# Two passes or one for small transposes, paired 64x64 products, a factor moved into u, and products of ones at the start of a hybrid decoder step

## The chip, the cores and the metric

The kernel runs on one core of a Trainium2 chip. The metric is the device time of one execution in microseconds (us), the median of repeated runs. The traces come from the hardware profiler, one execution each.

## The reference, cut to what matters

One layer of a decoder runs over 16 meta tokens and 512 prompt tokens, and over 8 sample sequences of 4 tokens (560 rows in all, width 1024):

```python
h = rms_norm(x, g_mix); proj = h @ w_in          # 1024 -> 8208
# branch A: GLU -> causal depthwise conv (31 taps) -> LayerNorm -> swish -> w_cout
# branch B: conv (4 taps) + SiLU on q, k, v, then for each of 8 heads, in chunks of L tokens:
M = beta[..., :, None] * einsum('id,jd->ij', k, k) * decay
A = tril(M, -1) + eye(L)
sol = triangular_solve(A, concat([v * beta, k * (beta * exp(G))]))   # value, kcum
attn = einsum('id,jd->ij', q, k) * decay
u = value - kcum @ S                              # S: state, key x value, 128 x 128
o = q_dec @ S + attn @ u
S = S * last + k_dec.T @ u
# o -> per-head RMSNorm * SiLU(z) -> w_dout
mix = sigmoid(gate_c) * conv_out + sigmoid(gate_d) * dn_out
x = x + mix @ w_o;  x = x + square(relu(rms_norm(x, g_mlp) @ w_up)) @ w_down;  y = rms_norm(x, g_final)
```

## The kernel before

**Big products.** Everything is kept transposed, channels on partitions. Each weight tile of 1024x128 is split into a rounded high part `wh` and a rest `wl` (both in fp32r), the activations likewise, and every product of the two is taken as high x high, high x low and low x high. These are the instructions of L613 (88 column tiles in the order of `gemm_order()`: k first, then the GLU pairs, q, v, z, the gates, then `do`, `co`, `wo`), of L2083 (`w_up`) and of L2234 (`w_down`). I call them main products. The weights come by SP's queue into `wraw`; ScalarE rounds them into `wh`. For tiles 12 to 71 ScalarE then writes -wh into `wl` (L579) and a DMA of GpSimd's queue adds the raw weights on top (L581); for the others VectorE subtracts (L585).

**Order.** A planner in the kernel (`Weaver`) writes the order of instructions of every engine when the program is built. The work is written as streams (Python generators) that yield one step at a time with its engine, an estimated cost and what it depends on; the planner always issues the step that could start first by its own clocks, and a priority breaks ties. Each engine then runs its list strictly in order. So a changed cost, dependency or priority moves instructions on all engines. `W.patience` holds back the convolution's VectorE steps (L1217), `tab` names the activation table that a ScalarE step needs.

**Start.** The eight tiles of x (`xs[:, k]`) arrive by DMA. Each is squared (L351 on GpSimd or VectorE, L354 on ScalarE), and TensorE sums the squares over partitions with a column of ones (`column_sums`, L877). Beside that, each tile is split into high and low (L401, L403), and the first four column tiles of the big product run on the split x before the norm is known. `warm` (L300) gives 20 products of ones at the very start and 12 at the end.

**Delta rule.** Gram products of k (L978) fill `KT`; VectorE inverts the 32x32 blocks (`solve`); `doubling` joins blocks to 64 and then to 128 with small products. Its last step has 32 products on rows 0 to 63 of the array (L1108), their move to SBUF, 32 products on rows 64 to 127 (L1119), and their move. For each head, `head_prep` brings v and k of the sample (`v4`, `k4`: L1411, L1413) and of the prompt (L1452, L1461) into token order, and `chain` goes through four chunks of 128 tokens: key and query times S (L1503, L1505), R on VectorE (L1509), T times R (L1518), eviction to `u` on ScalarE (L1520), `kd` times u and `at` times u (L1522, L1525), the new S on VectorE (L1529). A product in `head_post` (L1669) turns the sample's output back. `st["s"]` holds beta over the squared norm of k; `at` is attn times s (L1473, four instructions a head) and `kd` carries `st["sk"]` = s times the decay. `decode_state` updates the sample's states and loads the next by DMA (L1599).

Small products take plain fp32 operands. One such product is one row in the program's order and two rows (two passes) in the trace; the instruction `nc.tensor.transpose` is one row in both.

Of the kernel before, what the change touches and what calls it, by code (L numbers as in the profile page):

```python
# [22 lines left out]
NPH = NPOST // 2  # L23
# [84 lines left out]
class Weaver:  # L108
# [8 lines left out]
    def __init__(self):  # L117
        self.clk = {"pe": 0.0, "dve": 0.0, "act": 0.0, "pool": 0.0, "sp": 0.0}
        self.tab = None

        self.patience = 0.0
        self.streams = []
        self.n = 0
# [16 lines left out]
    def run(self):  # L140
        while self.streams:
            best = None
            moved = False
            for s in list(self.streams):
# [26 lines left out]
            if tab is not None:  # L171
# [18 lines left out]
def build(tc, i, o):  # L190
# [15 lines left out]
    with ExitStack() as ctx:  # L206
# [73 lines left out]
        A0, A1 = 12, 72  # L280
        SQ = "pdapadpd"
        NWARM, NTAIL = 20, 12
# [12 lines left out]
        def warm(n):  # L295

            b, kb, tb = yield from get_bank()
            w = ones[:].bitcast(mybir.dt.bfloat16)
            for _ in range(n):
                nc.tensor.matmul(b[:, 0:256], w[:, 0:128], w, start=True, stop=True)  # L300
            put_bank(kb, tb)

        def start():
# [39 lines left out]
            b, kb, tb = yield from get_bank()  # L343
            ta = [0.0] * 8
            for k in range(8):
# [9 lines left out]
                ta[k] = yield from column_sums(b, sq, ones[:, 0:32], t, tb, start=k == 0, stop=k == 7)  # L355
            b2, kb2, t = yield from sums_to_tokens(b, kb, M0[:, 6984:7112], M0[:, 7112:7160], ta[7],
# [235 lines left out]
        def gemm():  # L592
            src_of = {"do": "o", "co": "c", "wo": "m"}
            for idx, (kind, c) in enumerate(seq):
# [7 lines left out]
                for part in (0, 1):  # L602
                    for k in range(8):
# [6 lines left out]
                        for w, x in ((wls, hi),) if part else ((whs, hi), (whs, lo)):  # L610
                            t = yield op("pe", 2 * N * 0.4605e-3, tp, tk, tf)
# [377 lines left out]
        def kfin(t):  # L989
# [3 lines left out]
            t = yield op("dve", 0.2, t)  # L993
            nc.vector.tensor_tensor(st["sk"][:], st["s"][:], st["ed"][:], op=ALU.mult)
# [54 lines left out]
        def doubling(t0):  # L1049
# [56 lines left out]
            for m in range(32):  # L1106
                t = yield op("pe", 0.058, tn[m // 16], tb)
                nc.tensor.matmul(B[m // 8][64:128, m % 8, :], KT[0:64, m, 64:128], Tn[0:64, m, :], start=True, stop=True)  # L1108
                if m % 8 == 7:
                    tb_.append(t)  # L1110
            t1 = []
            for q in range(4):
                t1.append((yield from move(("act", "dve")[q % 2], 512, tb_[q], P2[q // 2][64:128, 8 * (q % 2):8 * (q % 2) + 8, :],
                                           B[q][64:128])))
            tb_ = []
            for m in range(32):
                h2 = m // 16
                t = yield op("pe", 0.058, *t1[2 * h2:2 * h2 + 2], *tc_[2 * h2:2 * h2 + 2])
                nc.tensor.matmul(B[m // 8][0:64, m % 8, :], P2[m // 16][64:128, m % 16, :], CTT[64:128, m, 64:128],  # L1119
                                 start=True, stop=True)  # L1120
                if m % 8 == 7:
                    tb_.append(t)
            for q in range(4):
# [264 lines left out]
        def head_prep(hh):  # L1388
# [21 lines left out]
            yield op("pe", 0.22, tv, tb4)  # L1410
            nc.tensor.matmul(b4[:96, 0:128], M2["v4"], ident, start=True, stop=True)  # L1411
            yield op("pe", 0.22, tv, tb4)
            nc.tensor.matmul(b4[:wk, 128:256], k4, ident, start=True, stop=True)  # L1413
# [14 lines left out]
            if hh == 5:  # L1428
                W.patience = 0.45
            t = yield op("dve", 0.15, t4)  # L1430
            nc.vector.scalar_tensor_tensor(at4[:48, 0:48], b4[:48, 384:432], st["s"][:48, hh, 4:5], D4[:, hh, :],
                                           op0=ALU.mult, op1=ALU.mult)
# [4 lines left out]
            nc.scalar.activation(kd[32:48, 4, :], b4[32:48, 128:256], AF.Copy, scale=st["sk"][32:48, hh, 4:5])  # L1437
# [3 lines left out]
            for r in (0, 32):  # L1441
                tx = yield op("act", 0.25, t4)
                nc.scalar.activation(kx[r:r + 32], b4[:32, 128:256], AF.Copy, scale=st["sk"][:32, hh, 4:5])
            t = yield op("dve", 0.2, tx)
            nc.vector.scalar_tensor_tensor(kx[64:96], b4[:32, 128:256], st["sk"][:32, hh, 4:5], kx[0:32].bitcast(F32),
# [1036 lines left out]
```

## Time and profile before

| | |
|---|---|
| median of 3 runs | 1069.06 us (1068.16 to 1070.02) |
| the profiled execution | 1068.65 us |
| its span, first to last instruction | 1066.9 us |
| TensorE busy | 1048.2 us (98% of the span) |
| VectorE busy | 769.4 us (72%) |
| ScalarE busy | 622.9 us (58%) |
| GpSimd busy | 148.1 us (14%) |

The span leaves out 1.75 us of the profiled execution. Matmuls are pipelined: a row's duration reaches from its start to the end of its last result, and neighbours overlap, so the cost of a product is read from the distance of the starts and not from its duration.

### The profile page before, as it was taken

To read this page: it belongs to the slowest core of one execution; us is meant where nothing else is said; L and a number is where in the kernel's file an instruction comes from. 1 tells how busy PE (TensorE), PEld (TensorE's weight loads), DVE (VectorE), ACT (ScalarE), POOL (GpSimd) and SP (SyncE) were. 2 spreads that over 40 slices of the span, in tenths; PEclk is the share of its full clock that TensorE was granted. 3 is DMA by queue.
4 is the path that set the end of the run, shared out by engine and by line. 5 is a ranking of instruction groups with operands and counts; after the bars stand their busy time and mean duration, and the time that the engine had idled before them with its cause. 6 is when DMAs were issued, how large, how long until landed. Compare 5 with 4: busy or idle time off the path is not lost.

```text
span 1066.9 us, 21819 instructions
## 1 busy us (share of the span) xinstructions
PE 1048.2 (98%) x8835; PEld 1026.1 (96%) x8835; DVE 769.4 (72%) x1360; ACT 622.9 (58%) x1285; POOL 148.1 (14%) x173
## 2 busy tenths in 40 slices
PE   8999999999999999999999999999999999999997
PEld 6988999999999999899999999999999999999996
DVE  5888879788889887788953355778657547746754
ACT  5677334668787878776358424578327426723741
POOL 2067311102211221122111000000000000000000
PEclk9999999999999999999999999999999999999998
DMA  6232687467576566667877522654365365346222
GB/s 213 82 89 70 124 178 164 87 148 161 139 172 164 143 137 156 164 166 182 187 163 158 179 84 91 163 153 117 109 177 129 100 153 149 94 124 164 80 61 84
DMA packets 57872, 145.55 MB, mean 136 GB/s; under 512 B 14612, under 2 KB 20140, under 8 KB 57772
## 3 DMA queue, kind: packets, MB, share of 16 engines
q1 hardware_dynamic: 46828, 104.32, 30.4%
q0 software_dynamic: 10944, 39.85, 23.2%
q8 instruction: 69, 1.13, 0.4%
q14 instruction: 31, 0.25, 0.1%
HBM read 135.14 MB, written 9.01 MB: 135 GB/s over the span
## 4 chain that ended last, share of the span: by engine, by line
PE 87%; DVE 5%; ACT 3%; DMA 3%; issue 2%; SPq 0%; POOL 0%; POOLq 0%; DVEq 0%; ACTq 0%
PE pg L613 42%; PE pg L2234 17%; PE bk L2083 15%; DVE acc L815 1%; DMA pre<-in_sq_dram 1%; DVE V L1217 1%; PE pg L2083 1%; PE bk L1419 1%; PE bk L1518 1%; PE bk L978 1%; DVE of L815 1%; PE bk L1522 1%; PE bk L1503 1%; DMA M<-in_xT_dram 1%; PE bk L1525 1%
## 5 line engine op out<-in xcount | busy, mean ns | idle before, releaser
L613 PE MATMUL pg<-R,wh 128*128 128x280 f32 (+2 forms) x1920 | 279.3, 295 | 1.0 <-ACT pre L803 1.0
L613 PEld LDWEIGHTS pg<-R,wh 128*128 128x128 f32 x1920 | 253.7, 189 | 3.9 <-issue 1.5
L1217 DVE SCALAR_TENSOR_TENSOR V<-V,vec,V 128x512 f32<-128x512 f32 x240 | 180.5, 781 | 2.2
L568 ACT ACTIVATE wh<-wraw 128x1024 fp32r<-128x1024 f32 (+1 forms) x89 | 93.4, 1049 | 94.3 <-PE pg L613 79.3
L613 PE MATMUL pg<-R,wl 128*128 128x280 f32 (+2 forms) x960 | 144.0, 294 | 0.3 <-issue 0.3
L613 PEld LDWEIGHTS pg<-R,wl 128*128 128x128 f32 x960 | 128.5, 189 | 1.8 <-issue 1.4
L581 POOL DMA_DIRECT2D wl<-in_w_dram x60 | 52.6, 876 | 343.8 <-ACT wl L579 252.5
L2014 ACT ACTIVATE whm<-RT 128x512 fp32r<-128x512 f32 x73 | 45.2, 625 | 53.0 <-PE pg L2234 34.8
L579 ACT ACTIVATE wl<-wh 128x1024 fp32r<-128x1024 f32 x60 | 63.5, 1058 | 14.8 <-PE pg L613 12.9
L1969 POOL DMA_DIRECT2D RT<-in_wu_dram x16 | 13.8, 865 | 381.6 <-DMA RT<-in_wu_dram 185.6
L2017 DVE TENSOR_TENSOR wlm<-RT,whm 128x512 fp32r<-128x512 f32 x73 | 49.8, 687 | 16.9 <-issue 8.4
L2234 PE MATMUL pg<-RD,whm 128*128 128x272 f32 (+2 forms) x272 | 57.7, 288 | 0.0
L2234 PE MATMUL pg<-K,whm 128*128 128x272 f32 (+2 forms) x272 | 57.6, 288 | 0.0
L2083 PE MATMUL bk<-R,whm 128*128 128x272 f32 x318 | 54.5, 288 | 0.0
L613 PE MATMUL pg<-K,wh 128*128 128x272 f32 x256 | 53.0, 289 | 0.2 <-DVE K L1766 0.2
L613 PE MATMUL pg<-RD,wh 128*128 128x272 f32 x256 | 53.2, 289 | 0.0
L2234 PE MATMUL pg<-RD,M 128*128 128x272 f32 x264 | 46.2, 288 | 0.0
L2014 ACT ACTIVATE whm<-wrawm 128x512 fp32r<-128x512 f32 x43 | 26.7, 623 | 32.6 <-PE pg L2234 29.7
L2083 PEld LDWEIGHTS bk<-R,whm 128*128 128x128 f32 x318 | 45.6, 189 | 0.0
L585 DVE TENSOR_TENSOR wl<-wraw,wh 128x1024 fp32r<-128x1024 f32 x28 | 35.1, 1253 | 13.5 <-ACT wh L568 9.5
L2234 PE MATMUL pg<-RD,wlm 128*128 128x272 f32 (+2 forms) x272 | 43.5, 289 | 0.0
L2234 PEld LDWEIGHTS pg<-K,whm 128*128 128x128 f32 x272 | 43.5, 188 | 0.0
(524 smaller groups left out, 2442.5 us busy)
## 6 DMA issues: line engine op xcount, KB each, us to landing
wraw<-in_w_dram SPq DMA_DIRECT2D x87, 512.0 KB, 3.8
wl<-in_w_dram POOLq DMA_DIRECT2D x60, 512.0 KB, 5.6
RT<-in_wu_dram SPq DMA_DIRECT2D x24, 512.0 KB, 5.2
RT<-in_wu_dram POOLq DMA_DIRECT2D x16, 512.0 KB, 7.3
wrawm<-in_wn_dram SPq DMA_DIRECT2D x16, 512.0 KB, 3.6
RT<-in_wn_dram SPq DMA_DIRECT2D x16, 512.0 KB, 3.5
M<-in_sd_dram SPq DMA_DIRECT2D x16, 256.0 KB, 3.4
out_osd_dram<-M SPq DMA_DIRECT2D x16, 256.0 KB, 3.8
```

Of the source, the lines that this page charges most:

```text
L568: nc.scalar.activation(wh[:, c[0]:c[1]], w[:, c[0]:c[1]], AF.Copy)
L579: nc.scalar.activation(wl, wh.bitcast(F32), AF.Copy, scale=-1.0)
L581: nc.gpsimd.dma_start(wl, i["w"][n].bitcast(F32R), accum_op=ALU.add)
L585: nc.vector.tensor_tensor(wl, w, wh.bitcast(F32), op=ALU.subtract)
L613: nc.tensor.matmul(pt[:, hf, 0:N], w[idx][:, k, :], x[:, off + hf * N:off + hf * N + N], start=k == 0 and not part and x is hi, stop=k == ...
L815: nc.vector.scalar_tensor_tensor(acc[:, 0:584], pr[:, q:q + 584], vcol(w + q), acc[:, 0:584], op0=ALU.mult, op1=ALU.add)
L1217: nc.vector.scalar_tensor_tensor(cc[:, 0:512], G[r][:, 16 + q:528 + q], vcol(w + q), cc[:, 0:512], op0=ALU.mult, op1=ALU.add)
L1969: nc.gpsimd.dma_start(rb, i["wu"][g][:, 1024:2048], accum_op=ALU.add)
L2014: nc.scalar.activation(hi, raw, AF.Copy)
L2017: nc.vector.tensor_tensor(lo, raw, hi.bitcast(F32), op=ALU.subtract)
L2083: nc.tensor.matmul(acc[an], w[:, kp, :], x, start=kp == 0 and not part and x is hi and m not in (3, 6, 7), stop=kp == 3 and part == 1, ski ...
L2234: nc.tensor.matmul(out, w[:, k % 4, :], x[:, a], start=n_ == 0 and x is hi, stop=n_ == len(STEPS) - 1)
```

## The change

It has these parts:

- `v4`, `k4` (for seven heads; the eighth has only 48 columns and stays) and the sample's output are turned by `nc.tensor.transpose` and no longer by a product with the identity.
- `doubling`'s last step is written in quarters of 8 products. The second products of quarter 0 alternate with the first products of quarter 2, those of quarter 1 with the first of quarter 3.
- The factor s leaves `at` and `kd` and is put on `u` when it is evicted; `at` becomes one instruction of 512 columns a head, the step that made `sk` goes.
- In `chain` the products with S of an odd chunk use other columns of the bank, so that they no longer wait for the output's eviction.
- `fill` puts four products of ones behind the column sums of each of the first six tiles of x.
- The planner counts 0.09 us more for a main product that follows a small product; `decode_state` gets priority -2 for 1; tiles 64 to 71 have `wl` from VectorE and not from ScalarE and a DMA; the reciprocals of the MLP's norm wait for an earlier product.

```diff
@@ Weaver.run
+                if eng == "pe":
+                    key, switch = (start, s[0], s[1]), False
+                    if best is None or key < best[0]:
+                        best = (key, s, eng, start, cost + (0.09 if self.small and tab == "main" else 0.0), tab)
+                    continue
...
-        A0, A1 = 12, 72
+        A0, A1 = 12, 64
-        NWARM, NTAIL = 20, 12
+        NWARM, NTAIL, NFILL = 20, 12, 6
...
+        def fill(b, n=4):
             w = ones[:].bitcast(mybir.dt.bfloat16)
             for _ in range(n):
                 nc.tensor.matmul(b[:, 0:256], w[:, 0:128], w, start=True, stop=True)
...
                 ta[k] = yield from column_sums(b, sq, ones[:, 0:32], t, tb, start=k == 0, stop=k == 7)
+                if k < NFILL:
+                    t = yield op("pe", 0.43, ta[k], tw_)
+                    fill(bw)
...
-            nc.vector.tensor_tensor(st["sk"][:], st["s"][:], st["ed"][:], op=ALU.mult)
@@ doubling
+            for q in (0, 1):
+                for m in range(8 * q, 8 * q + 8):
+                    yield from first(m, 0.116)
+                yield from keep(q)
+            for q in (2, 3):
+                for m in range(8 * q, 8 * q + 8):
+                    yield from first(m, 0.07)
+                    yield from second(m - 16, 0.07)
+                yield from keep(q)
+                yield from done(q - 2)
+            for q in (2, 3):
+                for m in range(8 * q, 8 * q + 8):
+                    yield from second(m, 0.116)
+                yield from done(q)
@@ head_prep
-            nc.tensor.matmul(b4[:96, 0:128], M2["v4"], ident, start=True, stop=True)
+            nc.tensor.transpose(b4[:96, 0:128], M2["v4"], ident)
-            nc.tensor.matmul(b4[:wk, 128:256], k4, ident, start=True, stop=True)
+            if wk > 64:
+                nc.tensor.transpose(b4[:wk, 128:256], k4, ident)
...
-                nc.scalar.activation(kd[:, j, :], b[:, 128 * j:128 * j + 128], AF.Copy, scale=st["sk"][:, hh, j:j + 1])
+                nc.scalar.activation(kd[:, j, :], b[:, 128 * j:128 * j + 128], AF.Copy, scale=st["ed"][:, hh, j:j + 1])
-            for j in range(4):
-                t1 = yield op("dve", 0.263, t)
-                nc.vector.scalar_tensor_tensor(at[:, j, :], b[:, 128 * j:128 * j + 128], st["s"][:, hh, j:j + 1],
-                                               Ds[hh][:, j, :], op0=ALU.mult, op1=ALU.mult)
+            t1 = yield op("dve", dve_c(512), t)
+            nc.vector.tensor_tensor(at, b.rearrange("p (t c) -> p t c", c=128), Ds[hh], op=ALU.mult)
@@ chain
+                ba, bu = (bx[:, 256:384], bx[:, 0:128]) if j % 2 else (bx[:, 0:128], bx[:, 256:384])
-                nc.scalar.activation(u, bx[:, 256:384], AF.Copy)
+                nc.scalar.activation(u, bu, AF.Copy, scale=st["s"][:, hh, j:j + 1])
...
-            W.spawn(decode_state(hh, tu), 1)
+            W.spawn(decode_state(hh, tu), -2)
@@ head_post
-            nc.tensor.matmul(b4[:, 0:48], ob[:, 4, :], ident[:, 0:48], start=True, stop=True)
+            nc.tensor.transpose(b4[:, 0:128], ob[:, 4, :], ident)
```

What the planner makes of it on TensorE's list at three places. First the start, where `bk` is the bank of the column sums and `pg` the first big product (`V` high, `RT` low part of x). Before:

```order
L877 MATMUL bk_38_149<-M_98,ones_71 32x128 x3
L877 MATMUL bk_38_149<-M_98,ones_71 32x176
L613 MATMUL pg_102<-V_37_148,wh_101 128x280 x2
L613 MATMUL pg_102<-RT_147,wh_101 128x280 x2
L877 MATMUL bk_38_149<-M_98,ones_71 32x128 x3
L877 MATMUL bk_38_149<-M_98,ones_71 32x176
```

And of the change (L895 is the former L877, L631 the former L613, L313 the products of ones):

```order
L895 MATMUL bk_38_149<-M_98,ones_71 32x128 x3
L895 MATMUL bk_38_149<-M_98,ones_71 32x176
L313 LDWEIGHTS ones_71
L313 MATMUL bk_39_150<-ones_71 128x256
L313 LDWEIGHTS ones_71
L313 MATMUL bk_39_150<-ones_71 128x256
L313 LDWEIGHTS ones_71
L313 MATMUL bk_39_150<-ones_71 128x256
L313 LDWEIGHTS ones_71
L313 MATMUL bk_39_150<-ones_71 128x256
L631 MATMUL pg_102<-V_37_148,wh_101 128x280 x2
L631 MATMUL pg_102<-RT_147,wh_101 128x280 x2
```

Four products of ones now stand between the sums of a tile and what follows. Second, the last step of `doubling` (`KT` and `P2` lie in `M`, the inverse in `RT`, each `bk` is a quarter). Before:

```order
L613 MATMUL pg_2349<-R_29_97,wh_2082 128x280 x4
L1108 MATMUL bk_155_2339<-M_751 64x64 x8
L1108 MATMUL bk_156_2340<-M_751 64x64 x8
L1108 MATMUL bk_157_2341<-M_751 64x64 x8
L1108 MATMUL bk_158_2342<-M_751 64x64 x8
L613 MATMUL pg_2349<-R_29_97,wh_2082 128x280 x12
L1119 MATMUL bk_155_2339<-RT_750,M_751 64x64 x8
L1119 MATMUL bk_156_2340<-RT_750,M_751 64x64 x8
```

And of the change (L1128 is the former L1108, L1133 the former L1119):

```order
L631 MATMUL pg_2261<-R_29_97,wh_2102 128x280 x18
L1128 MATMUL bk_158_2392<-M_815 64x64 x8
L631 MATMUL pg_2261<-R_29_97,wh_2102 128x280 x2
L1128 MATMUL bk_159_2393<-M_815 64x64 x8
L631 MATMUL pg_2261<-R_29_97,wh_2102 128x280 x2
L1128 MATMUL bk_160_2394<-M_815 64x64
L1133 MATMUL bk_158_2392<-RT_814,M_815 64x64
L1128 MATMUL bk_160_2394<-M_815 64x64
L1133 MATMUL bk_158_2392<-RT_814,M_815 64x64
```

Two blocks of 32 products have become six blocks: two of 8, two of 8 pairs, two of 8, with main products between them. Third, the first steps of a head's preparation and a post step, where the change issues as many rows as before but other instructions. Of the change:

```order
L1443 MATMUL bk_168_2600<-cst_68,M_2542 96x128
L1446 MATMUL bk_168_2600<-cst_68,kq_26_93 96x128
L1450 MATMUL bk_168_2600<-kq_26_93 96x48
L631 MATMUL pg_2493<-R_29_97,wl_2260 128x274 x2
L1454 MATMUL bk_168_2600<-ones_71,M_2542 128x1 x4
L1454 MATMUL bk_168_2600<-ones_71,M_2542 96x1
...
L631 MATMUL pg_3182<-R_29_97,wl_3065 128x280 x6
L1702 MATMUL bk_198_3285<-cst_68,M_2542 128x128
L631 MATMUL pg_3182<-R_29_97,wl_3065 128x280 x6
```

Here L1443 and L1446 stand for the former L1411 and L1413, and L1702 for L1669, whose moving operand had 48 columns. In all of TensorE's list a main product follows a small one 183 times before and 186 times in the change.

## Rows read from the trace of the kernel before

**Rows 1.** The page: busy time of TensorE, and its busy tenths over 40 slices.

```profile
PE 1048.2 (98%) x8835; PEld 1026.1 (96%) x8835; DVE 769.4 (72%) x1360; ACT 622.9 (58%) x1285; POOL 148.1 (14%) x173
...
PE   8999999999999999999999999999999999999997
```

**Rows 2.** Waits of TensorE: engine, line, waited for: us in total, times, longest.

```profile
PE bk L1503 <- ACT M L1537: 2.1, 2, 1.5
PE bk L1546 <- DMA M<-in_sd_dram: 1.1, 1, 1.1
PE pg L613 <- ACT pre L803: 1.0, 1, 1.0
PE bk L755 <- ACT D L715: 0.8, 1, 0.8
PE bk L755 <- ACT RD L764: 0.6, 1, 0.6
```

**Rows 3.** A window: stretch, length, busy PE, PEld, DVE, ACT, POOL, clock, DMA.

```profile
360.00:400.00 40.00, 39.99 (x341) 38.72 (x340) 33.98 (x74) 33.18 (x102) 10.36 (x9) 1.00 0.65 148
```

**Rows 4.** Timeline of TensorE in head 0's preparation: start, duration, instruction, count.

```profile
206.00 0.38 PE L1411 MATMUL bk<-cst,M 128*96 128x128 f32 x2
206.22 0.38 PE L1413 MATMUL bk<-cst,kq 128*96 128x128 f32 x2
...
209.48 0.60 PE L1452 MATMUL bk<-cst,M 128*128 128x128 f32 x4
209.84 0.37 PE L613 MATMUL pg<-R,wh 128*128 128x274 f32 x1
```

**Rows 5.** Timeline of TensorE at a product of `head_post`.

```profile
289.92 0.32 PE L1669 MATMUL bk<-cst,M 128*128 128x48 f32 x2
290.05 2.05 PE L613 MATMUL pg<-R,wh 128*128 128x280 f32 x14
```

**Rows 6.** Timeline of TensorE around the first products of the last doubling step.

```profile
190.01 0.29 PE L613 MATMUL pg<-R,wh 128*128 128x280 f32 x1
190.23 3.94 PE L1108 MATMUL bk<-M 64*64 64x64 f32 x64
194.10 1.82 PE L613 MATMUL pg<-R,wh 128*128 128x280 f32 x12
```

**Rows 7.** Timeline of TensorE in an earlier doubling step, two quadrants in turn.

```profile
178.83 0.19 PE L1077 MATMUL bk<-M 32*32 32x32 f32 x1
178.83 0.19 PE L1075 MATMUL bk<-M 32*32 32x32 f32 x1
178.86 0.19 PE L1077 MATMUL bk<-M 32*32 32x32 f32 x1
```

**Rows 8.** Windows of the start, columns as in rows 3.

```profile
11.60:14.90 3.30, 3.30 (x20) 2.49 (x18) 3.30 (x4) 3.25 (x6) 1.35 (x1) 0.50 1.02 396
15.00:25.30 10.30, 10.30 (x114) 8.21 (x112) 4.70 (x8) 4.10 (x13) 1.23 (x2) 1.00 0.23 68
```

**Rows 9.** Timeline of TensorE: products of ones at the end of the program.

```profile
1055.89 1.47 PE L300 MATMUL bk<-ones 128*128 128x256 bf16 x12 [0.42 <-DVE V L2301]
```

**Rows 10.** Timelines of TensorE and ScalarE: one chunk's way from T times R to `kd` times u.

```profile
355.91 0.39 PE L1518 MATMUL bk<-M,RT 128*128 128x128 f32 x2
...
357.11 0.39 PE L1522 MATMUL bk<-M 128*128 128x128 f32 x2
...
356.34 0.28 ACT L1520 ACTIVATE M<-bk 128x128 f32<-128x128 f32 x1 [0.37 <-PE bk L1518]
```

**Rows 11.** Groups by line in the heads' stage (200 to 480 us), ScalarE and VectorE.

```profile
L1512 ACT ACTIVATE M<-bk,st_eG 128x128 f32<-128x128 f32 x24 | 8.8, 365 | 9.4 <-DVE M L1509 9.4
L1520 ACT ACTIVATE M<-bk 128x128 f32<-128x128 f32 x32 | 8.7, 271 | 4.8 <-PE bk L1518 4.6
...
L1629 DVE TENSOR_TENSOR M<-bk,M 128x512 f32<-128x512 f32 x14 | 9.6, 684 | 2.4 <-ACT M L1626 2.4
L1473 DVE SCALAR_TENSOR_TENSOR M<-bk,st_s,RD 128x128 f32<-128x128 f32 x32 | 9.5, 344 | 2.0 <-PE bk L1469 2.0
```

More of the change, by code (lines that the diff above doesn't have):

```diff
@@ L119, in __init__ @@
         self.tab = None
+        self.small = False
         self.patience = 0.0
@@ L170, in run @@
             _, s, eng, start, cost, tab = best
-            if tab is not None:
+            if eng == "pe":
+                self.small = tab != "main"
+            elif tab is not None:
                 self.tab = tab
@@ L343, in start @@
             b, kb, tb = yield from get_bank()
+            bw, kw, tw_ = yield from get_bank()
             ta = [0.0] * 8
@@ L610, in gemm @@
                         for w, x in ((wls, hi),) if part else ((whs, hi), (whs, lo)):
-                            t = yield op("pe", 2 * N * 0.4605e-3, tp, tk, tf)
+                            t = yield op("pe", 2 * N * 0.4605e-3, tp, tk, tf, tab="main")
                             for hf in range(2):
@@ L1105, in doubling, with first, second, keep @@
             tb = max(x[2] for x in bks)
-            for m in range(32):
-                t = yield op("pe", 0.058, tn[m // 16], tb)
+            t1, tb_ = [None] * 4, [None] * 4
+            def first(m, cost):
+                tb_[m // 8] = yield op("pe", cost, tn[m // 16], tb)
                 nc.tensor.matmul(B[m // 8][64:128, m % 8, :], KT[0:64, m, 64:128], Tn[0:64, m, :], start=True, stop=True)
[L1109 to L1119, printed above, removed]
+            def second(m, cost):
+                q = m // 8
+                tb_[q] = yield op("pe", cost, t1[q], *tc_[2 * (m // 16):2 * (m // 16) + 2])
+                nc.tensor.matmul(B[q][0:64, m % 8, :], P2[m // 16][64:128, m % 16, :], CTT[64:128, m, 64:128],
                                  start=True, stop=True)
-                if m % 8 == 7:
-                    tb_.append(t)
-            for q in range(4):
+            def keep(q):
+                t1[q] = yield from move(("act", "dve")[q % 2], 512, tb_[q], P2[q // 2][64:128, 8 * (q % 2):8 * (q % 2) + 8, :],
+                                        B[q][64:128])
+            def done(q):
                 t = yield from move(("act", "dve")[q % 2], 512, tb_[q], CTT[0:64, 8 * q:8 * q + 8, 64:128], B[q][0:64], -1.0)
@@ L1531, in chain @@
                     to = yield op("dve", 0.2, to)
-                    nc.vector.tensor_tensor(ob[:, j, :], bx[:, 0:128], tm, op=ALU.add)
+                    nc.vector.tensor_tensor(ob[:, j, :], ba, tm, op=ALU.add)
                 else:
@@ L1536, in chain @@
                     to = yield op("act", 0.17, to)
[L1537 removed]
+                    nc.scalar.activation(ob[:, j, :], ba, AF.Copy)
                 S = Sn
@@ L1885, in mlp_norm @@
             evac_done(n, t)
-            yield wait(("upm", 4, 4))
+            yield wait(("upm", 3, 2))
             for q in range(4):
@@ L2231, in dn_product @@
                 for w, x in ((wl, hi),) if part else ((wh, hi), (wh, lo)):
-                    t = yield op("pe", sum(a.stop - a.start for _, a in parts) * 0.4605e-3, tp, tk, tf)
+                    t = yield op("pe", sum(a.stop - a.start for _, a in parts) * 0.4605e-3, tp, tk, tf, tab="main")
                     for out, a in parts:
```

50 lines of the change are left out of this document (25 added, 25 removed).

## The prediction, written before the changed kernel ran

> **What bounds the kernel now.** I read the page first, for the shares: TensorE is busy for 1048.2 of 1066.9 us, and in 38 of 40 slices its tenths stand at 9 [rows 1]. VectorE and ScalarE stay under three quarters. So the time is TensorE's list plus its gaps, and an edit counts only if it takes something off that list, shortens a wait of TensorE or makes one. Next come TensorE's waits. Above half a microsecond there are few, and those inside the program that I use later come to 5.6 us: 2.1 for the products with S (L1503), 1.1 for a sample's state from DMA (L1546), 1.0 for a big product behind ScalarE (L613), 0.8 and 0.6 for the decay products (L755) [rows 2]. Third, a window of the heads' stage, where the change makes most of its edits: VectorE 34 and ScalarE 33 of 40 us, TensorE all 40 [rows 3]. These engines have some 6 us of slack in 40, so the sources of small products are ready just in time there. Last, timelines at each place touched. In them the reader is to look at the first column, since distances of starts are what a product costs.
>
> **Transposes.** A product with the identity takes two passes: L1411 starts at 206.00 and L1413 at 206.22. A transpose takes one: the four of L1452 reach from 209.48 to 209.84, 0.09 us each. The rows of the instructions say so too, with x2 for one product and x4 for four transposes [rows 4]. The change turns 8 `v4` and 7 `k4` products into transposes, 15 × 0.11 = 1.65 us. The eight of L1669 stand alone between main products, and there the row is cheaper: from its start to the next main product 0.13 us, for both passes of 48 columns [rows 5]. It becomes one pass of 128 columns. Its gain is at most 0.13 and at least nothing, if a lone pass costs as much; I take 0.10, since the way in and out seems to be overlapped already, times 8 = 0.8. Sum **-2.45 us** (bounds -1.65 to -2.7).
>
> **Doubling.** The first block of 32 products reaches from 190.23 to 194.10, where the next main product starts. 64 passes lie in it: 3.94 less some 0.22 for the last pass's own duration (it is 0.19 for a 32x32 one [rows 7]), over 63 distances, is 0.059 us a pass [rows 6]. All 64 products are 128 passes. No row of before has 64x64 products of two quadrants in turn. The nearest is an earlier doubling step with 32x32 quadrants in turn: both rows of a pair start at 178.83, the next pair at 178.86 [rows 7]. There a partner costs nothing. In the change 16 pairs hide 16 products, or 32 passes, 32 × 0.059 = -1.89 us. Against that, there are six blocks where there were two. The edge of a block into main products reads 0.22 us on the way in, 190.01 to 190.23 [rows 6], which is 0.09 above the 0.13 that a main product costs from start to start (2.05 us for 14 [rows 5], less the 0.29 of a single one [rows 6], over 13 distances). On the way out, the last of the 64 passes is done with its distance at 190.23 + 64 × 0.059 = 194.01, and the main product starts at 194.10: 0.09 as well. Four more blocks at 0.18 cost 0.72. Net **-1.2 us**; bounds are -1.9 (edges free) and +0.7 (no overlap of the pairs).
>
> A rule speaks against this part. The Trainium skill, page "TensorEngine Tiling (Array Packing)", section "Key Properties", says that a change of the tiling mode, not just of the tile, drains TensorE; six blocks mean twelve changes for four. The trace agrees that an edge costs something, with the 0.09 read above, and no run yet shows whether a full drain can be longer.
>
> **Products of ones.** At the program's end twelve of them last 1.47 us; less 0.27 for the last one's lag that is 0.109 each [rows 9]. The change adds 24, or 2.6 us. Before, TensorE's clock in 11.6 to 14.9 stood at 0.50, the lower of its two levels (1.2 GHz), after stretches in which it waited for squares and copies, while VectorE and ScalarE were busy for 3.30 and 3.25 of 3.30 us; from 15.0 on it is 1.00 [rows 8]. So until 14.9 TensorE follows the split of x, and fills there fall mostly into its idle time. If the fills raise the clock earlier, a few of the 20 products in that stretch come sooner; but what follows needs the norm, which comes from VectorE and ScalarE. Bounds: -0.8 (a quarter of the slow stretch) and +0.9 (the eight fills of the fifth and sixth tile, 8 × 0.109, are all on the path). I take **0**.
>
> **s in u.** On ScalarE the eviction to `u` gets a factor per row. The row of such an eviction is L1512, 365 ns against the 271 ns of L1520 [rows 11], +0.094 us for 32 chunks and 8 samples, 3.8 us of ScalarE. On VectorE four instructions of 344 ns become one of 512 columns, as L1629 has at 684 ns: 8 × (4 × 0.344 - 0.684) = 5.5 us less [rows 11]. Is the eviction on the path? T times R starts at 355.91, ScalarE evicts from 356.34 to 356.62, and `kd` times u starts at 357.11, with main products between [rows 10]. That leaves some 0.49 us of cover, and +0.094 fits in it. The one `at` instruction comes once a head, before the chain starts, so the chain's first product with `at` waits for 0.684 us of VectorE and no longer for 0.344; it stands several products into the chain. **0 us**; without the cover it would be up to 3.8 us.
>
> **The rest.** For tiles 64 to 71 ScalarE loses eight instructions and GpSimd's queue eight transfers, VectorE gets eight subtractions; main products are waited for by nobody there who is late. The bank's halves swapped in odd chunks take away a wait that the waits don't show. The state's step at -2, the reciprocals one product earlier, the dropped `sk`: each moves work that main products hide now. **0 us** together. The planner's 0.09 moves small products into longer bundles or out of them; TensorE's list has 183 returns from small to main before and 186 in the change, so it saves no edges. 0 too, but see the rivals.
>
> **Sum.** -2.45 - 1.2 = -3.65 us. The profiled execution had 1068.65, of which the span is 1066.9; 1068.65 - 3.65 = 1065.0. That execution lay 0.41 below the median of 1069.06, so the median is forecast at **1065.4 us**. What a measurement of this kernel can tell from no change is about 0.2%, or 2.1 us.
>
> **Rivals.** *Faster, waits go too.* The waits for the decay products (0.8 + 0.6), for ScalarE ahead of L613 (1.0) and for the sample's state (1.1) add to 3.5 us [rows 2]. The earlier priority of the state's step, which issues the next state's load, speaks to the last one, and a less loaded VectorE to the others. If all go, 1065.4 - 3.5 = 1061.9. Against it: other waits take their place easily when the order of everything changes.
>
> *No gain.* TensorE is shortened by 3.65 us, but the engines behind it are not, and those 6 us of slack in 40 [rows 3] are a mean; saved passes turn into waits for VectorE, ScalarE or weights. Waits of 5.6 us [rows 2] would need to grow by two thirds. It gives some 1069.
>
> *Slower, the chain loses its cover.* The planner now believes that each return from small to main costs 0.09 us, on some 140 of the 186 returns (those in the heads' stage), and plans the other engines' steps by a TensorE list 140 × 0.09 = 12.6 us longer than before. The real return, as L1669 shows with 0.13 us for two passes and the way back [rows 5], need not cost that much. Then TensorE arrives earlier than planned at products whose source is not ready. With `u` 0.094 later on top, a hop from T times R to `kd` times u is short by 0.19 us at worst, over 40 hops 7.6 us: 1065.4 + 7.6 = 1073.0. It comes out slower than before by more than a measurement's 2.1 us once the 40 hops wait for 0.14 us each (5.7 us). The 0.49 us of cover speaks against it; the full VectorE and ScalarE of that stage speak for it.
>
> **Chances.** The forecast 0.50, with a range of its own of 1063.7 to 1068.1 (1069.06 with the best bounds, -2.7 - 1.9 - 0.8, and with the worst of transposes and doubling, -1.65 + 0.7); the faster rival 0.20; no gain 0.18; the slower rival 0.12. The forecast and the faster rival end below 1066.9, that is 0.2% under the median, but for 0.05 of the former; the no-gain case ends within 0.2% but for 0.01, and 0.01 of the slower rival does too: faster 0.65, same 0.23, slower 0.12. The range reaches from 1061.0, a little below the faster rival, to 1070.0, above the no-gain case, and leaves out most of the slower rival and a tail of the faster one, together under 0.2.
>
> **What would show it.** Each step has its place in the profile after. The rows of L1443, L1446 and L1702 should have one pass each and 0.09 to 0.12 us to the next start. L1128 and L1133 should start in pairs, 0.12 us from pair to pair of two passes each, in six blocks with edges near 0.09 us. The clock in 11.6 to 14.9 tells what the fills do, and the start of the first product behind the norm tells whether that counts. `u` should last some 365 ns with no wait of TensorE for it above half a microsecond in total, and `at` be one instruction of 684 ns. I am wrong on the forecast if TensorE's waits for the evictions to `u`, for R or for the state's update grow to some 3 us or more, if pairs start 0.06 us apart from partner to partner, or if the edges cost several tenths.

## The result and the profile after

The changed kernel takes 1077.36 us in the median of 5 runs (1075.65 to 1081.27), the kernel before 1069.84 on the same chip. The ratio is 1.0079 with a 95% interval of 1.0057 to 1.0101: slower by 8 us, where 1065.4 was forecast. The profiled execution is the slowest of the five (1081.27); a second profile (e1) spans 1078.4 us. I therefore call structural only what both show.

The busy times on the page of the changed kernel, against [rows 1]:

```profile
PE 1054.0 (98%) x8836; PEld 1029.1 (95%) x8836; DVE 771.8 (71%) x1343; ACT 620.2 (57%) x1278; POOL 140.6 (13%) x165
```

TensorE's five longest waits (engine, line, waited for: us in total, times, longest), against [rows 2]:

```profile
PE bk L1551 <- ACT M L1545: 3.9, 3, 3.5
PE pg L631 <- DVE R L482: 2.7, 3, 1.5
PE bk L1108 <- issue: 2.0, 1, 2.0
PE pg L2267 <- DVE V L2283: 1.7, 1, 1.7
PE pg L2116 <- DVE V L2175: 1.5, 1, 1.5
```

L1551 is T times R in the chain, and its wait is for a ScalarE eviction. The R that L631 waits for is another one: the tiles with the split of the normalized x (L482). L1108 is a 32x32 product of `doubling`. Of these five, before has only the first, with 0.3 us. They add to 11.8 us; the waits of before for the products with S and for in_sd, 3.2 us [rows 2], are gone or small (0.4). They cost more than their length, because the clock falls behind some of them. Windows (columns as in [rows 3]) just behind the waits for R and inside the 32x32 products:

```profile
52.00:56.00 4.00, 3.05 (x12) 2.79 (x13) 4.00 (x5) 1.02 (x2) 2.61 (x2) 0.61 0.23 78
56.00:60.00 4.00, 4.00 (x20) 4.00 (x19) 3.54 (x5) 3.47 (x10) 0.00 (x0) 0.54 0.04 7
196.00:200.00 4.00, 4.00 (x49) 3.96 (x40) 2.98 (x5) 1.18 (x2) 0.00 (x0) 0.57 0.44 88
```

In 56 to 60 TensorE is busy all the time and starts 20 products, where e1 starts 32 and 33 in the two stretches of 4 us from 54 on, with a granted clock of 1.00. Near 0.5 is the lower of the two levels, 1.2 GHz. The fall is not the same in every execution: e1 is the same program with the same waits for R, and there the clock falls behind the stall at L1108 and the wait at L1551 but not behind R. Up to 1040 us the clock's records have the lower level for 13.7 us in the changed kernel, 10.2 in e1, 3.4 before and none in e2. At half the clock half of that is lost, which is an estimate of 5 to 7 us out of the 17 to 18 between e2's profile and these two.

Where the time goes is easiest seen by counting main products, of which all kernels have the same 7104 in nearly the same order. How much later (us) than in the profile of before the n-th starts, counted from the traces' records (an earlier small product in the order also makes the n-th later: ahead of 300, the changed kernel and e5 have 39 small passes more than before and e6 has 15; ahead of 900 it is 24, the products of ones, and none):

| n | 300 | 900 | 1200 | 2700 | 4350 | 7050 |
|---|---|---|---|---|---|---|
| place | R split | before the Gram part | after doubling | after the heads | in the MLP | near the end |
| after | 9.3 | 4.2 | 5.6 | 9.5 | 9.5 | 13.1 |
| after again (e1) | 6.3 | 3.2 | 5.8 | 9.6 | 9.5 | 11.6 |
| e2: neither | -0.8 | -0.8 | -1.6 | -5.9 | -5.9 | -4.7 |
| e5: products, no 0.09 | 6.0 | 2.2 | 8.1 | 3.4 | 3.4 | 5.0 |
| e6: 0.09, no products | 10.3 | 5.3 | 6.6 | 11.3 | 11.3 | 13.7 |
| e7: products, order kept | -0.1 | -0.0 | 2.0 | -3.4 | -3.4 | 1.0 |
| e12: the same, fewer passes | 0.1 | 0.1 | -0.1 | -4.5 | -4.5 | -2.5 |

### The profile page after: what moved, and what is told of

It is laid out like the page before. It is cut to its first block, busy times and chain, and to the rows that moved or that the text cites. A ratio compares the mean times of both kernels' runs of the same rounds, so it can differ in the third digit from the quotient of the medians.

```text
span 1079.5 us, 21784 instructions
## 1 busy us (share of the span) xinstructions
PE 1054.0 (98%) x8836; PEld 1029.1 (95%) x8836; DVE 771.8 (71%) x1343; ACT 620.2 (57%) x1278; POOL 140.6 (13%) x165
## 4 chain that ended last, share of the span: by engine, by line
PE 89%; DVE 3%; ACT 3%; DMA 3%; issue 2%; POOL 1%; SPq 0%; POOLq 0%; DVEq 0%; ACTq 0%
PE pg L631 46%; PE pg L2267 17%; PE bk L2116 14%; DMA RT<-in_wu_dram 1%; PE bk L996 1%; PE bk L1503 1%; PE bk L1555 1%; PE bk L1551 1%; POOL um L1649 1%; DMA M<-in_sd_dram 1%; PE bk L1454 1%; PE bk L1558 1%; DMA M<-in_xT_dram 1%; PE bk L1536 0%; PE pg L2116 0%
## 5 line engine op out<-in xcount | busy, mean ns | idle before, releaser
L631 PE MATMUL pg<-R,wh 128*128 128x280 f32 (+2 forms) x1920 | 282.9, 296 | 2.8 <-DVE R L482 2.7
L631 PEld LDWEIGHTS pg<-R,wh 128*128 128x128 f32 x1920 | 256.7, 191 | 6.8 <-DVE R L482 3.4
L1249 DVE SCALAR_TENSOR_TENSOR V<-V,vec,V 128x512 f32<-128x512 f32 x240 | 173.3, 750 | 3.4 <-ACT V L1240 1.1
L631 PE MATMUL pg<-R,wl 128*128 128x280 f32 (+2 forms) x960 | 144.4, 297 | 0.0
L631 PEld LDWEIGHTS pg<-R,wl 128*128 128x128 f32 x960 | 129.7, 191 | 0.8 <-issue 0.6
L599 POOL DMA_DIRECT2D wl<-in_w_dram x52 | 45.6, 877 | 340.4 <-ACT wl L597 244.4
L603 DVE TENSOR_TENSOR wl<-wraw,wh 128x1024 fp32r<-128x1024 f32 x36 | 45.6, 1266 | 35.6 <-PE pg L631 14.4
L597 ACT ACTIVATE wl<-wh 128x1024 fp32r<-128x1024 f32 x52 | 55.1, 1059 | 12.5 <-PE pg L631 10.2
L2267 PE MATMUL pg<-RD,whm 128*128 128x272 f32 (+2 forms) x272 | 57.7, 288 | 1.7 <-DVE V L2283 1.7
L2267 PE MATMUL pg<-K,whm 128*128 128x272 f32 (+2 forms) x272 | 57.7, 288 | 0.0
L2116 PE MATMUL bk<-R,whm 128*128 128x272 f32 x318 | 54.5, 288 | 0.0
L631 PE MATMUL pg<-K,wh 128*128 128x272 f32 x256 | 53.2, 289 | 0.2 <-DVE K L1799 0.2
L631 PE MATMUL pg<-RD,wh 128*128 128x272 f32 x256 | 53.0, 288 | 0.0
L2267 PE MATMUL pg<-RD,M 128*128 128x272 f32 x264 | 46.2, 288 | 0.0
L2116 PEld LDWEIGHTS bk<-R,whm 128*128 128x128 f32 x318 | 45.5, 188 | 0.0
L2267 PEld LDWEIGHTS pg<-RD,whm 128*128 128x128 f32 x272 | 43.4, 188 | 1.9 <-issue 1.9
L2267 PE MATMUL pg<-RD,wlm 128*128 128x272 f32 (+2 forms) x272 | 43.4, 288 | 0.0
```

What stands on the lines that cost most here:

```text
L597: nc.scalar.activation(wl, wh.bitcast(F32), AF.Copy, scale=-1.0)
L599: nc.gpsimd.dma_start(wl, i["w"][n].bitcast(F32R), accum_op=ALU.add)
L603: nc.vector.tensor_tensor(wl, w, wh.bitcast(F32), op=ALU.subtract)
L631: nc.tensor.matmul(pt[:, hf, 0:N], w[idx][:, k, :], x[:, off + hf * N:off + hf * N + N], start=k == 0 and not part and x is hi, stop=k == ...
L1249: nc.vector.scalar_tensor_tensor(cc[:, 0:512], G[r][:, 16 + q:528 + q], vcol(w + q), cc[:, 0:512], op0=ALU.mult, op1=ALU.add)
L2116: nc.tensor.matmul(acc[an], w[:, kp, :], x, start=kp == 0 and not part and x is hi and m not in (3, 6, 7), stop=kp == 3 and part == 1, ski ...
```

## The experiments

My theory after reading the two traces was "order": the planner, given other costs, writes another order, and its waits stand in every execution. The rivals were late transfers in one execution, and a chain of hops that s in u makes longer. All results, against the kernel before on the same chip:

| run | median us | ratio, 95% interval |
|---|---|---|
| e1 changed kernel again | 1079.26 | 1.0094 (1.0073 to 1.0114) |
| e2 without 0.09 and products | 1063.51 | 0.9951 (0.9935 to 0.9967) |
| e3 reciprocals as before | 1079.56 | 1.0097 (1.0081 to 1.0114) |
| e4 s in `at` as before | 1077.83 | 1.0078 (1.0049 to 1.0107) |
| e5 without 0.09 | 1070.23 | 1.0014 (0.9994 to 1.0033) |
| e6 without products | 1082.96 | 1.0128 (1.0107 to 1.0149) |
| e7 e2 and products, order kept | 1068.99 | 0.9986 (0.9970 to 1.0001) |
| e8 e2, s in `at` as before | 1064.61 | 0.9958 (0.9942 to 0.9973) |
| e9 GpSimd held | 1081.81 | 1.0121 (1.0100 to 1.0141) |
| e10 e2, 10 wide products first | 1063.55 | 0.9942 (0.9927 to 0.9958) |
| e11 e2, 44 short products first | 1067.01 | 0.9971 (0.9958 to 0.9985) |
| e12 e7 with fewer, wider products | 1063.89 | 0.9943 (0.9927 to 0.9960) |
| e13 state's step at 1 | 1077.78 | 1.0079 (1.0053 to 1.0106) |
| e14 the parts kept | 1063.21 | 0.9942 (0.9919 to 0.9964) |

**e1.** 

> The changed kernel once more, for a second profile. Theory 'order' (the waits come from the new order of instructions, so they stand in every execution): the wait for the split of R near main product 160 (2.7 us, with a lower clock behind it) and the one for L2283 (1.7 us) are there again, and the start is again some 4 us behind the kernel before at main product 900. Theory 'transfers' (the profiled execution met late transfers): the waits behind a load of in_sq (3.5 us at L1551), for RT from in_wu (1.5 us at L2116) and the stall inside the 32x32 block (2.0 us) are gone, and the span is near 1074 us rather than 1079.5.

The waits for R (2.7), at L1551 (3.5), at L1108 (2.0) and at L2267 (1.7) stand there again to 0.4 us. Only the one at L2116 is gone. "Order" holds for the waits; "transfers" holds for the last alone. The clock behind the waits for R does not come again, which is why main product 300 is 6.3 us late and not 9.3.

**e2.** The hunk of `Weaver.run` and `NFILL` undone, all else kept.

```diff
-                        best = (key, s, eng, start, cost + (0.09 if self.small and tab == "main" else 0.0), tab)
...
-                if k < NFILL:
-                    t = yield op("pe", 0.43, ta[k], tw_)
-                    fill(bw)
```

> The changed kernel without the planner's 0.09 us and without the 24 products of ones. The decay product L728 goes back from behind main product 224 to behind 384 in the order. Theory 'order at the start': the loss of 4 us ahead of the heads is gone, time 1077.4 - 4 = 1073.4. Theory 'longer chain' (s in u makes the hops of the chain late): no change, 1077.

0.9951, some 14 us below the changed kernel, far more than the 4 us expected: these two parts carry the whole loss and hide a gain of 5.3 us (3.5 to 6.9 by the interval). Its longest wait is again one at the start (2.0, a column sum for ScalarE, 1.7 before); the second to the seventh:

```profile
PE bk L2355 <- POOL ncol L2351: 1.2, 1, 1.2
PE bk L300 <- POOL ones L307: 1.0, 1, 1.0
PE bk L755 <- ACT D L715: 1.0, 1, 1.0
PE pg L613 <- ACT pre L803: 1.0, 1, 1.0
PE pg L2098 <- DVE V L2157: 0.9, 1, 0.9
PE bk L1533 <- ACT M L1527: 0.8, 1, 0.8
```

**e3.** `("upm", 3, 2)` back to `("upm", 4, 4)`. 

> The changed kernel with the MLP's reciprocals after the product they waited for before. TensorE's order stays the same. If the reciprocals' new place on VectorE makes L2267 wait for L2283 (1.7 us), that wait goes: 1077.4 - 1.9 = 1075.5 and the step behind main product 4800 is 0 and not 2.0 us. If the wait has another cause (the subtraction ahead on VectorE waiting for TensorE), it stays: 1077.4.

This edit changes nothing: the planner writes the same instructions in the same order on every engine, so e3 is the changed kernel a third time, and the earlier place of the reciprocals, listed among the parts of the change, moves nothing. The third profile has the wait for R (2.2), the one at L1551 (3.6), the stall at L1108 (1.5) and a lower clock behind the waits for R again. The wait at L2267 stays at 1.7. It stands in every trace that has the planner's 0.09 and in none without.

**e4, e8.** s back in `at` and `kd`, in the changed kernel and in e2.

```diff
-                nc.scalar.activation(u, bu, AF.Copy, scale=st["s"][:, hh, j:j + 1])
+                nc.scalar.activation(u, bx[:, 256:384], AF.Copy)
```

> The changed kernel with s in at and kd, u evicted without a factor, the bank's halves not swapped. Theory 'longer chain': the loss in the heads' stage (4 us, where 2.5 us of gain were expected) goes, 1077.4 - 6 = 1071. Theory 'order': waits elsewhere stay, the time moves by less than 2 us, 1075.5 to 1079.

> The kernel without the planner's 0.09 us, without the products of ones, and with s in at and kd as before: left are transposes, doubling, the state's step, tiles 64 to 71 and the reciprocals. By the prediction s in u costs and gives nothing: 1063.5, give or take 1. Theory 'longer chain': faster, 1061. Theory 's in u is what gave the gain beyond 3.65': slower, 1065.2.

No change that the intervals show in either, 1.0078 to 1.0079 and 0.9958 to 0.9951. As the cause of the loss the "longer chain" falls. That s in u is free in the heads is not shown by it: in e8's profile main product 2700 comes 4.0 us earlier than in e2's (-9.9 against -5.9), and a later wait of 2.8 us of L613 for ScalarE (L1314), with a granted clock of 0.50 in 591 to 594, takes 6 us back before main product 3600. In e4 2700 is 8.8 us late, like the changed kernel (9.5).

**e5, e6.** The two parts one at a time. 

> The changed kernel without the planner's 0.09 us; the products of ones stay, with their 0.43 us a group in the planner's clock. In the order the decay product L728 stands behind main product 220, as in the changed kernel. Theory 'either part moves the decay work ahead of the split of R': the start costs again 3 to 4 us, the time is near 1063.5 + 4 + what the order does in the heads, 1067 to 1072. Theory 'the planner's 0.09 is the cause': the start is as without both, 1063.5 to 1065.

> The changed kernel without the products of ones; the planner's 0.09 us stays. From main product 300 on TensorE's order is that of the changed kernel. Theory 'order': as slow as the changed kernel, 1076 to 1079, with the waits for R (L482), at L1551 and L2283. Theory 'the products of ones are the cause': near 1064.

With e2 and the changed kernel this is a square: neither 0.9951, products alone 1.0014, the 0.09 alone 1.0128, both 1.0079. The planner's 0.09 is the larger: +1.8% without the products, +0.65% with them. The products cost 0.6% alone and give 0.5% back beside the 0.09. Either part moves the decay products from behind main product 384 to 220 or 224, and each shows a delay of 6 to 10 us at main product 300, of which 2 to 5 are left at 900. e6 is 4 us above the range that its expectation gave to "order". (e5's 8.1 at 1200 is a stall of 5.5 us in the 32x32 products, of the kind that e7 to e12 explain.) The hunk of `Weaver.run` does one thing more than the 0.09: on TensorE it no longer holds back the streams of rank 2.5 and 4. That is not the price: with only the 0.09 set to 0 and the rest of the hunk kept, the planner writes e5's order for TensorE, product by product.

**e7.** `fill` called without the planner's step, so that the order is that of e2.

```diff
-                    t = yield op("pe", 0.43, ta[k], tw_)
                     fill(bw)
```

> The kernel without the planner's 0.09 us and with the 24 products of ones put in without a step of the planner, so that the order is that of the kernel without both (L728 behind main product 384). This prices the products themselves: by the prediction between -0.8 and +0.9 us against 1063.5, that is 1062.7 to 1064.4. If they held TensorE up by their full 2.6 us, 1066.1.

+0.35% or 3.7 us by the ratios (1.3 to 6.1 with their intervals), 5.5 by the medians: nominally more than the 2.6 us that the products themselves take. Its executions spread widely, 1062.1 to 1069.7, and the profiled one (1069.15) is one of the longer. At main product 900, at 158 us, it is only 0.7 us behind e2; the rest comes later, long after the last added product. Its two longest waits:

```profile
PE pg L2106 <- DVE V L2165: 2.7, 1, 2.7
PE bk L1096 <- issue: 2.0, 1, 2.0
```

"issue" means that TensorE waited for nothing that the profile shows. Counted in the records, the long gap in 180 to 200 us stands at the same place of TensorE's list in nine of the ten traces so far: in front of its 1747th pass (counted from 0), twice also 1619, 128 passes earlier, whatever instruction that is. In the changed kernel:

```profile
193.53 0.19 PE L1108 MATMUL bk<-RT,M 32*32 32x32 f32 x1
195.74 0.21 PE L1108 MATMUL bk<-RT,M 32*32 32x32 f32 x1 [1.97 <-issue]
```

In the middle of a run of like products with no operand pending. From pass 1619 to 1747 it takes 3.48 us before, 3.51 after, 3.54 in e1, e6 and e7, though 12 of the passes between are main products before (1.6 us) and none is in the others, where all are products of some 0.02 us. That led to "pieces of 128 passes": TensorE's instructions come in pieces, and a piece of short products is used up before the next has come.

**e10 to e12.** The same columns of ones as more or fewer products.

```diff
-        NWARM, NTAIL = 20, 12
+        NWARM, NTAIL = 10, 12
...
+                    nc.tensor.matmul(b.rearrange("p (o c) -> p o c", o=2), w[:, 0:128],
+                                     w.rearrange("p (o c) -> p o c", o=1).to_broadcast([P, 2, 256]), start=True, stop=True)
```

> The kernel without the planner's 0.09 us and the products of ones behind the sums; besides, the 20 products of ones of 256 columns at the very start become 10 of 512. Nothing else moves, but every later product stands 10 passes earlier in TensorE's list. Theory 'TensorE's list comes in pieces of 128 passes' (the stalls that wait for nothing stand at pass 1619 and 1747 in eight of nine traces, whatever instruction that is): ten more main products fall before pass 1747 and the 32x32 block less, so the stall there (0.8 us) shrinks by up to 1.2 us to nothing, 1063.5 - 1 to -2 = 1062. Rival 'the stall belongs to the 32x32 products or the transfers of that time': no change, 1063.5.

> As the one before, but the 20 products of ones at the very start become 44 of 116 columns: 24 passes more, as many as the change adds, and none behind the sums. Theory 'pieces of 128 passes': pass 1747 falls into the 32x32 block and the stall is 2.0 us as in the kernel with the 24 products, with a lower clock behind it, 1063.5 + 3 = 1066.5. Rival 'the products behind the sums cost the time themselves': 1063.5.

> The kernel with the products of ones behind the sums and the order kept, but as two of 512 columns a tile for four of 256, and the ten of 512 at the start: the same columns, and a list that is two passes longer than without them, not 24. Theory 'pieces of 128 passes': the stall at pass 1747 is again 0.6 to 1.0 us and the time 1063.5, give or take 1. Rival 'the products themselves cost time': 1067 to 1069 as before.

The stall follows the count. 24 passes more at the very start (e11) give 1.9 us at pass 1747 and 1067.0; the same columns behind the sums in two passes more (e12) give 0.9 at 1619, 0.3 at 1747 and 1063.9; ten fewer (e10) leave 0.2. In time e10's gain over e2 (0.9942 to 0.9951) lies inside the intervals. So the products' time is free, as forecast, and their number is not. e7 and e11 also wait 2.7 and 2.9 us for VectorE behind the load of in_wu, the kernels with neither the 24 passes nor the 0.09 for 0.9 to 1.2, and e5, with the 24 passes, for 1.3; why, is open.

The pieces themselves stand in the traces. The page of the changed kernel has, among its DMA queues (packets, MB, share):

```profile
q8 instruction: 69, 1.13, 0.4%
```

That is 69 packets of 16 KB for 8836 passes and their weight loads, one for some 128 passes. In all sixteen traces each stall of 0.1 us or more in front of pass 1619 or 1747 (in e9 of 1748) ends 1.2 to 1.5 us after one of these packets has landed; in the changed kernel the packet starts at 193.12 and lands at 194.44, and pass 1747 starts at 195.74. The packet for 1747 starts 0.7 to 1.6 us behind pass 1619 where the stall is 2.0 us or less, but 3.0 us behind it in e4 (stall 3.8), 4.0 in e9 (3.1) and 4.8 in e5 (5.5). So the longest stalls are late transfers, on top of a piece that is used up fast. What made these packets late is not shown.

**e9.** Two 128x1 copies on GpSimd that read the last tile of R stand ahead of the decay's products there, one in each of two streams; one of them:

```diff
+                    th = yield wait(("h", 7))
+                    t = yield op("pool", 0.1, t, th)
+                    nc.gpsimd.tensor_copy(T("hold", [P, 1])[:], h[:, 1, 7, 0:1].bitcast(F32))
```

> The changed kernel with GpSimd's products for the decay held back by a small copy (128x1) that reads the last split tile of the normalized x, so that they don't run beside the split on VectorE; the planner's order behind the start moves too, so only the start is read. If GpSimd's work beside VectorE is what slows the split (three instructions of L482 in 3.53 us, a subtraction of 2.06 in place of 1.22 us), L482 takes 0.73 us again, R is ready 2.2 us earlier, TensorE's wait for R falls from 2.7 to 1 us or less and the delay at main product 300 against the kernel before falls from 8.5 or 9.3 us to 4 to 6. If the split is slow for another reason, L482 stays near 1.2 us each and the wait near 2.7.

VectorE's timeline of the changed kernel and, second, of e9:

```profile
47.46 2.06 DVE L603 TENSOR_TENSOR wl<-wraw,wh 128x1024 fp32r<-128x1024 f32 x1
49.44 0.82 DVE L716 TENSOR_SCALAR st_neG<-st_eG 128x40 f32<-128x40 f32 x1
50.18 3.53 DVE L482 TENSOR_TENSOR R<-M,R 128x560 fp32r<-128x560 f32 x3
```

```profile
46.87 1.22 DVE L603 TENSOR_TENSOR wl<-wraw,wh 128x1024 fp32r<-128x1024 f32 x1
48.01 0.18 DVE L716 TENSOR_SCALAR st_neG<-st_eG 128x40 f32<-128x40 f32 x1
48.10 2.04 DVE L482 TENSOR_TENSOR R<-M,R 128x560 fp32r<-128x560 f32 x3
```

The same instructions on the same tiles take 6.41 us beside GpSimd's products and 3.44 without. The Trainium skill ("GPSIMD Engine Reference", "Specifications") says that GpSimd shares its SBUF interfaces with VectorE, and that VectorE's instructions in a 2-port perf mode or with two SBUF inputs contend; the trace agrees for L603 and L482, which have two. L716, which has one such input, is slowed too (0.18 to 0.82); in which mode it runs no run shows. TensorE's wait for R is gone in e9 and main product 300 is 3.2 us late, not 9.3 or 6.3. But at main product 900 nothing is left of that (4.3 us late, against 4.2 and 3.2), and the kernel as a whole stays slow (1.0121). The edit also makes the planner move other work. So GpSimd beside VectorE makes this wait; that it costs the kernel time is not shown.

**e13.** `decode_state` back at priority 1. 

> The changed kernel with the priority of the state's step back at 1; the planner's 0.09 us and the products of ones stay. On SP's queue the state's transfers (in_sd, out_osd) and those of the convolution's cache (in_sc) no longer stand between a tile's eviction and the load of in_sq. Theory 'the queue in front of in_sq makes ScalarE and then T times R wait (3.2 to 3.6 us in three traces, and a lower clock behind it)': this wait is gone, 1077.4 - 4.8 = 1072.6; the waits for R, inside the 32x32 block and for L2283 stay. Rival 'the 0.09 us alone makes the heads late': another wait of the same size stands in the heads, 1076 to 1079.

The wait stood behind a load in the changed kernel, on SP's queue and on ScalarE:

```profile
294.26 0.34 SPq L1632 DMA_DIRECT2D M<-in_sd_dram  x1
294.69 0.98 SPq L1230 DMA_DIRECT2D Ex<-in_sc_dram  x2
295.76 0.38 SPq L1667 DMA_DIRECT2D out_osd_dram<-M  x1
296.20 0.42 SPq L799 DMA_DIRECT2D pre<-in_sq_dram  x1
```

```profile
295.77 1.06 ACT L597 ACTIVATE wl<-wh 128x1024 fp32r<-128x1024 f32 x1
300.60 0.20 ACT L821 ACTIVATE pre<-pg 128x32 f32<-128x32 f32 x1 [3.77 <-DMA pre<-in_sq_dram]
...
301.91 0.36 ACT L1545 ACTIVATE M<-bk,st_eG 128x128 f32<-128x128 f32 x1
```

L821 needs 28 KB that were asked for behind four larger transfers; L1545 stands behind L821, and T times R (L1551) waits for it. In e13 the wait is gone and main product 2700 is 6.1 us late, not 9.6. But the medians don't show it (1.0079 again; its executions reach from 1075.9 to 1080.3). So the queue made that wait, as expected; the 4.8 us that were to go with it don't show, and whether it costs the kernel 3.4 us stays open.

**e14.** 

> The version that the runs so far point to: transposes, paired doubling, s in u, the state's step at -2 and ten products of 512 columns at the start; without the planner's 0.09 us, the products of ones behind the sums, the move of tiles 64 to 71 and the earlier reciprocals. If the wait of TensorE for VectorE behind the load of in_wu (1.0 to 2.9 us at the same product in seven traces, none in the kernel before) comes with one of the last two, 1063.5 - 1.2 = 1062.3; if not, 1063.5.

1063.21, 0.9942: with e10 and e12 (0.9942, 0.9943) the fastest, 6 us faster than before, though the intervals don't tell it from e2. The wait behind in_wu is still 0.9, so the move of tiles 64 to 71 doesn't make it; the edit of the reciprocals moves nothing here either.

## Why the prediction was wrong

**The step that failed** stands under "The rest" and "Products of ones": the planner's 0.09 at 0 and the products at 0. I counted returns from small to main (183 and 186; the two traces have 183 both), found no edge saved, and took that for the price. The price of a planner's cost is the order that it writes on every engine. By the square the 0.09 costs 0.65% beside the products and 1.8% without them, 7 and 19 us; both parts together cost 1.3%, 14 us. The order shown with the change has the products of ones in place; the decay products, 160 main products earlier, and GpSimd beside VectorE there were not considered. How the 14 us divide among the new waits is only in part shown: taking away the wait for R (e9) or the one at L1551 (e13) did not make the kernel faster.

**The slower rival** named the right part and the wrong place. It put 7.6 us on 40 hops of the chain. The wait for `u` (L1555 for L1553) is 0.6 us in three places. The waits that came with the new order stand at the split of R, in the 32x32 products, behind one load of 28 KB, and at L2267.

**Products of ones.** Their own time is nothing, within the bounds (e12 against e2). What was missing is their number, 24 passes, which left no main product among the 128 passes ahead of 1747, and their step in the planner, which moves the decay products (e5, 1.0014, against e7, 0.9986). The clock in 11.6 to 14.9 is 1.00 in the changed kernel, but in e2 without them too, so they did not raise it; whether before always has the 0.50 of [rows 8] is not shown.

**Transposes** were right. In the changed kernel:

```profile
216.52 0.27 PE L1443 MATMUL bk<-cst,M 128*96 128x128 f32 x1
216.63 0.27 PE L1446 MATMUL bk<-cst,kq 128*96 128x128 f32 x1
216.74 0.29 PE L1450 MATMUL bk<-kq 128*96 128x48 f32 x2
...
294.07 0.27 PE L1702 MATMUL bk<-cst,M 128*128 128x128 f32 x1
294.10 0.76 PE L631 MATMUL pg<-R,wl 128*128 128x274 f32 x4
```

0.11 for 0.22 [rows 4], and 0.03 to the next main product for 0.13 [rows 5]; six of the eight of L1702 have that. The 0.13 was not the whole price of a lone product, though: in both kernels the main product behind it takes some 0.21 to the next start and not 0.13. The difference of 0.10 is not touched by that.

**Doubling** was right in the mechanism and too large in its sum. Pairs lie on top of each other:

```profile
201.39 0.53 PE L631 MATMUL pg<-R,wh 128*128 128x280 f32 x2
201.85 1.14 PE L1128 MATMUL bk<-M 64*64 64x64 f32 x16
202.92 0.52 PE L631 MATMUL pg<-R,wh 128*128 128x280 f32 x2
203.37 0.27 PE L1128 MATMUL bk<-M 64*64 64x64 f32 x1
203.38 0.27 PE L1133 MATMUL bk<-RT,M 64*64 64x64 f32 x1
203.47 0.22 PE L1128 MATMUL bk<-M 64*64 64x64 f32 x1
203.48 0.22 PE L1133 MATMUL bk<-RT,M 64*64 64x64 f32 x1
```

A partner starts 0.01 us after its pass. But what a block costs beside its passes is 0.46 - 2 × 0.13 = 0.20 from the first main product to the block and 1.07 - 16 × 0.059 = 0.13 from the block to the next: 0.33 a block for 0.18. Of the 0.20, 0.10 fall on the first main product behind a block, which takes 0.23 to the next start for 0.13. My reading left that out, though before has it too (194.10 to 194.34). Four more blocks cost 1.3, not 0.72, and the net is -0.6, not -1.2. The drain that the Trainium skill states ("TensorEngine Tiling (Array Packing)", "Key Properties") fits that better than my reading of the edge did; the trace agrees that a block costs something at its edges, 0.33 us, and does not show of what it consists.

**s in u** was right in its rows: `u` takes 366 ns, `at` one instruction of 684 ns, and TensorE's wait for `u` is 0.6 us. That it is 0 in the time is so within the intervals (e4, e8); e8's heads leave up to 4 us open.

```profile
L1553 ACT ACTIVATE M<-bk,st_s 128x128 f32<-128x128 f32 x32 | 11.6, 366 | 2.4 <-PE bk L1551 2.3
...
L1506 DVE TENSOR_TENSOR M<-bk,RD 128x512 f32<-128x512 f32 x8 | 5.5, 684 | 1.3 <-PE bk L1503 1.3
```

**The rest of the sum** stood in the number, partly by luck: without the two parts e2 has -5.3 us where -3.65 was forecast, but transposes and doubling as measured give only -2.45 - 0.6 = -3.05. The remaining 2.2 are not assigned. The waits at L1503 and for in_sd (3.2 us, part of them the faster rival's) are not in e2's list, and the lower clock that before had in 11.6 to 14.9 is not in e2 either.

## What to carry to other kernels

Where a planner writes the order, a cost in its table is not an estimate but an edit of every engine's list. Price it by the order that comes out, on the engines that wait, and try it alone. In a kernel whose main engine is 98% busy, look first at what a new wait does beyond its length, since the clock behind it counts too. And a count of instructions is a cost of its own where short ones stand in a row. Last, compare the written orders before a run is read: e3's edit had written the same program.

## What was not expected of the hardware

- TensorE's list stalls at fixed pass numbers, 1619 and 1747, 128 apart ("issue" in the profile). Where all 128 passes between were short, some 0.02 us each, the stall was 1.5 to 5.5 us (nine traces of seven kernels); with 10 to 28 main products among them it was 1.0 us or less, but 3.1 in e9. From one number to the other it took 2.9 us or more in every trace, and each stall ended 1.2 to 1.5 us after a packet of 16 KB of the queue that the page calls "instruction" had landed.
- GpSimd's products slow VectorE's beside them by 1.7 times: 1.22 to 2.06 us, 0.68 to 1.18 us (e9 against the changed kernel).
- The same waits of the same program were followed by a lower clock in one execution and not in another: behind waits for R of 2.7 us in all the granted clock was 0.61 and 0.54 for 8 us in the first profile, and 1.00 in e1.
